# Weight columns 8 and 16 bytes apart in the two projections around a cross-attention

## The chip, the cores and the metric

One core of a Trainium2 chip runs the whole kernel. The metric is the device time of one execution in microseconds; the kernel before takes 1947.67 us, the median of three runs (1947.66 to 1947.83).

## The reference

One decoder block over 1024 tokens of width 1024: two recurrent branches, merged and projected, then cross-attention to 256 memory tokens, then a gated feed-forward network. The change concerns the cross-attention, which is, cut to what matters:

```python
def mem_cross_attention(n, m, w_xq, w_xkv, w_xo):
    q = (n @ w_xq).reshape(Bsz, S, XATTN_HEADS, XATTN_HEAD_DIM)
    k, v = jnp.split(m @ w_xkv, 2, axis=-1)
    ...
    s = jnp.einsum('bshd,bmhd->bhsm', q, k).astype(jnp.float32) * (XATTN_HEAD_DIM ** -0.5)
    p = jax.nn.softmax(s, axis=-1).astype(v.dtype)
    o = jnp.einsum('bhsm,bmhd->bshd', p, v).reshape(Bsz, S, D_MODEL)
    return o @ w_xo
```

`w_xq` and `w_xo` are 1024 x 1024 float32; there are four heads of 256.

## The kernel before, in words

Everything is float32 in and out, and matmuls run on fp32r operands. To keep precision each operand is split in two: `split` (L226) writes a high part with a ScalarE copy (L227) and a low part with VectorE's subtraction (recorded at L73, the line of a helper that records every two-input operation). A product is then three matmuls: high by high, high by low, low by high. The matmul itself is recorded at L51, a transpose at L55.

Five square matrices pass through one routine: the two branches' up-projections, the merge's output, the query projection (`w_xq`) and the attention's output projection (`w_xo`). Their weights are the left operand, the one that TensorE loads; class `Left` prepares them (L1190-1219). Each matrix is fetched in four DMAs of 256 columns into `raw` (L1197). From `raw` come eight tiles of 128 columns a matrix, one for each block of 128 output channels; a tile named `wd` holds both parts of the 8 blocks of the contraction, 128 partitions x 2 parts x 8 blocks x 128 columns (`slot(...)`, L1209). There are two such buffers, used in turn, so a tile is split into the buffer that the tile before the last leaves. In the text "weight tile" means one `wd`.

`dense` (L1236-1253) runs one matrix: for each of the 8 output blocks and each half of the tokens (512) it adds up 24 matmuls, 8 blocks x 3 products, in one PSUM bank `acc` (L1249); four such banks rotate. A tile is therefore read by 2 x 24 = 48 matmuls of 128 x 512, each with a weight load of its own (128 columns), and a matrix takes 384. The result goes to `post`, which empties the bank: in the query projection (`dense(3)`, L1407) a split into the attention's `hl` operand, in the output projection (`dense(4)`, L1537) the residual sum (`ga`), a store to memory, the statistics of the norm (`ssum`, `sq`) and a scaled copy `o` (L1534) for the feed-forward network, whose first operands (`B11h` and others) are split there too.

Between the two lies the attention (`Att`, L1412-1460): for each head and half, scores with 256 columns a matmul (`acc<-kvhl,hl`), the softmax on ScalarE and VectorE (`pe`, L1440), transposes on TensorE (`bank<-ident,pe`), a split of the transposed probabilities (`phl`), the sum over values (`bank<-phl,kvhl`), and a split of the result into `hl`, the right operand of the output projection.

The order is not written by hand: a scheduler places each instruction on its engine from its own estimate of times and from priorities. Splits of weights and the `post` steps are issued under `ahead` (L131), which raises their priority by 200 (L37). So TensorE already runs some matmuls of the output projection between the last heads' steps. Within an engine the instructions run in the order placed, each after the semaphores that it waits for.

Of the kernel before, what the change touches and what calls it, by code (L numbers as in the profile page):

```python
# [16 lines left out]
P = 128  # L17
TOK = 1024
D = 1024
NB = D // P  # L20
# [58 lines left out]
def block_kernel(ctx: ExitStack, tc: tile.TileContext, t: dict, out: bass.AP):  # L79
    nc = tc.nc  # L80
    now = [0.0]
    PE, ACT, SP = Tensor(nc.tensor, now), nc.scalar, nc.sync
# [39 lines left out]
    def acc():  # L122
        return ps.tile([P, 512], F32, name="acc", tag="acc", bufs=4)

    def bank(dt=F32):
        return ps.tile([P, 512], dt, name="bank", tag="bank", bufs=4)
# [7 lines left out]
    half = lambda j: slice(j * HALF, (j + 1) * HALF)  # L134
# [8 lines left out]
    def slot(key, shape=(P, 2, TOK), dt=F32, name="sl"):  # L143
        pl, n = slots[key]
        return pl.tile(list(shape), dt, name=name, tag="sl", bufs=n)
# [80 lines left out]
    def split(src, hi, lo, e=None):  # L226
        ACT.activation(hi, src, AF.Copy)  # L227
        sub(e or DVE, lo, src, hi)
# [5 lines left out]
    class Operands:  # L234
# [20 lines left out]
        def upto(s, n):  # L255

            while s.done < min(n, 7 * s.kh):
                next(s.steps)
                s.done += 1
# [287 lines left out]
    for k in range(NB):  # L547
        p = bank()
# [640 lines left out]

    class Left:  # L1190

        def __init__(s, mats):
            s.seq, s.raw, s.w, s.ring = [(W, u) for W in mats for u in range(4)], [], [], []
# [8 lines left out]
        def upto(s, n):  # L1204
            while len(s.w) < min(n, 2 * len(s.seq)):
                u, i = divmod(len(s.w), 2)
                s.load(u + 1)
                if len(s.w) < 2:
                    s.ring.append(slot("m", (P, 2, NB, P), F32R, name="wd"))  # L1209
                w = s.ring[len(s.w) % 2]  # L1210
                with ahead():
                    split(s.raw[u][:, :, i * P:(i + 1) * P], w[:, 0], w[:, 1])
                s.w.append(w)
                if i:
                    s.load(u + 3)

# [19 lines left out]
    def dense(no, ins, post, pre=lambda o, j: None, js=JS):  # L1236

        todo = [(o, j) for o in range(NB) for j in (js if o + 1 < NB else js[::-1])]
        got = [pre(*x) for x in todo[:2]]
        for n, (o, j) in enumerate(todo):  # L1240
            w = left[NB * no + o]
            if n + 2 < len(todo):
                got.append(pre(*todo[n + 2]))
            cur = got[n]
            p = acc()
            m = 0
            for k in range(NB):
                for a, b in ((0, 0), (0, 1), (1, 0)):
                    PE.matmul(p, w[:, a, k], ins[k][:, b, half(j)], start=m == 0, stop=m == 3 * NB - 1)  # L1249
                    m += 1  # L1250
            with ahead():
                post(o, j, p, cur)
            yield
# [122 lines left out]

    early = presum()
    run(dense(0, i_ys, post_ys, lambda o, j: gate(gs_d, o, j)), (fetch_gated(yg_d, sr_d, i_yg), 1.0), (waiting(early, 12), 1.0))
    run(dense(1, i_yg, post_yg, lambda o, j: (gate(gg_d, o, j), quad(ysg_d, o * P, 0, j))), (early, 1.1))
    run(dense(2, i_wo, residual(h1_d, s1, "norm_xattn", put_xq, 0.5), quad_of(xT_d)), (early, 1.1))  # L1380


# [88 lines left out]
    for n in range(len(at) + 2):  # L1471
        a = at[n] if n < len(at) else None
        b = at[n - 1] if 0 < n <= len(at) else None
# [277 lines left out]
```

## Time and profile before

| What | Value |
|---|---|
| timed runs, median (lowest, highest) | 1947.67 us (1947.66, 1947.83) |
| the profiled execution, its span | 1949.0 us |
| TensorE busy | 1916.2 us, 98% of the span |
| VectorE busy | 1298.5 us, 67% |
| ScalarE busy | 845.8 us, 43% |
| matmuls on weight tiles (all five matrices) | 1920, mean record 390 ns |
| their weight loads | 1920, mean record 188 ns |
| splits of weight tiles, ScalarE | 40, mean 1057 ns |
| splits of weight tiles, VectorE | 40, mean 1323 ns |
| query projection | about 1067 to 1156 us of the span |
| attention, with the output projection's start | 1156 to 1220 us |
| output projection, to its last matmul | 1198 to 1297 us |

The profiled execution's own time is its span, since nothing runs outside it in the record. PE is TensorE's matmul side, PEld its weight loads, which run beside the matmul before them; DVE is VectorE, ACT ScalarE, POOL GpSimd. A line of a view names the line of the code, the engine, the operation, and its operands as out<-in with their shapes. Matmuls' records overlap, so their mean is longer than the step from one to the next; the step is read from a row of the timeline, which gives a run of matmuls from the first start to the last end.

### The profile page before, as it was taken

What the parts mean: (1) busy time and instruction counts of PE and PEld (TensorE: products, weight loads), DVE (VectorE), ACT (ScalarE), POOL (GpSimd) and SP (SyncE); (2) the same over time, 40 slices, a digit from 0 to 9 for tenths busy, and PEclk for the clock granted to TensorE, in tenths of its full rate; (3) what the DMA queues carried; (4) which work ended last, traced back from release to release, by engine and by line L of the source; (5) the groups of instructions that cost most, each with busy time, mean ns of one, the idle gap of its engine ahead of it and who ended that gap; (6) DMA issues with size and microseconds to landing.
All of it is one profiled execution on the core that took longest, in us unless ns stands there. A gap on an engine that the chain in (4) does not pass through costs nothing.

```text
span 1949.0 us, 26264 instructions
## 1 busy us (share of the span) xinstructions
PE 1916.2 (98%) x9776; PEld 1615.6 (83%) x9776; DVE 1298.5 (67%) x1873; ACT 845.8 (43%) x1485; POOL 557.8 (29%) x428
## 2 busy tenths in 40 slices
PE   7999999999999999999999999999999999999998
PEld 7998787888878888788887888888888888888888
DVE  7766879877776764655534237677777777766566
ACT  7534564655553444643223235444333333345243
POOL 0012334345543231022433000006445544320002
PEclk9999999999999999999999999999999999999999
DMA  9423383446553653997675201442233224177463
GB/s 341 144 93 101 130 307 107 152 161 186 174 173 123 198 167 124 348 346 270 226 269 164 82 22 44 140 141 82 90 126 110 82 100 144 42 271 239 157 224 126
DMA packets 237875, 317.98 MB, mean 163 GB/s; under 512 B 16538, under 2 KB 156036, under 8 KB 237748
## 3 DMA queue, kind: packets, MB, share of 16 engines
q1 hardware_dynamic: 236020, 310.01, 47.4%
q10 hardware_dynamic: 1728, 6.29, 0.8%
q8 instruction: 77, 1.26, 0.3%
q14 instruction: 50, 0.41, 0.1%
HBM read 215.27 MB, written 100.99 MB: 162 GB/s over the span
## 4 chain that ended last, share of the span: by engine, by line
PE 43%; DMA 3%; POOL 2%; DVE 1%; issue 1%; ACT 1%; POOLq 0%; SPq 0%; DVEq 0%; ACTq 0%
PE acc L51 38%; PE bank L51 4%; DMA pre<-in_w_ffn_out_dram 1%; POOL pre L73 1%; DMA down_d<-pre 1%; PE bank L55 1%; POOL ssum L73 0%; DVE hl L73 0%; POOL sa L73 0%; DMA h_d<-ga 0%; DMA ga<-vm_d 0%; DVE wd L73 0%; ACT wd L227 0%; ACT sq L493 0%; DVE phl L73 0%
## 5 line engine op out<-in xcount | busy, mean ns | idle before, releaser
L51 PE MATMUL acc<-hl,wd 128*128 128x512 f32 x1920 | 440.4, 390 | 3.6 <-DVE wd L73 2.0
L51 PEld LDWEIGHTS acc<-hl,wd 128*128 128x128 f32 x1920 | 359.6, 188 | 80.7 <-DVE wd L73 3.3
L73 DVE TENSOR_TENSOR wlo<-raw,whi 128x512 fp32r<-128x512 f32 x272 | 236.4, 875 | 103.6 <-ACT whi L227 103.5
L227 ACT ACTIVATE whi<-raw 128x512 fp32r<-128x512 f32 x272 | 169.5, 629 | 247.6 <-PE acc L51 201.0
L73 DVE TENSOR_TENSOR o<-acc,o 128x512 f32<-128x512 f32 (+1 forms) x256 | 172.6, 676 | 108.8 <-PE acc L51 95.4
L51 PE MATMUL acc<-fs 128*128 128x512 f32 (+1 forms) x792 | 155.7, 356 | 0.1
L51 PEld LDWEIGHTS acc<-fs 128*128 128x128 f32 x792 | 130.7, 189 | 20.8 <-issue 0.5
L73 DVE TENSOR_TENSOR fs<-fr,fs 128x1024 fp32r<-128x1024 f32 (+1 forms) x84 | 98.9, 1217 | 36.5 <-ACT fs L227 36.4
L227 ACT ACTIVATE fs<-fr 128x1024 fp32r<-128x1024 f32 (+1 forms) x84 | 79.2, 982 | 95.9 <-PE acc L51 31.2
L73 POOL TENSOR_TENSOR raw<-raw,sa 128x512 f32<-128x512 f32 x44 | 57.1, 1297 | 207.8 <-DVE wlo L73 207.8
L73 POOL TENSOR_TENSOR sa<-raw 128x512 f32<-128x512 f32 x43 | 69.6, 1619 | 107.0 <-DMA raw<-in_w_in_dram 78.9
L227 ACT ACTIVATE whi<-sa 128x512 fp32r<-128x512 f32 x96 | 59.6, 626 | 93.7 <-PE acc L51 92.3
L73 DVE TENSOR_TENSOR wlo<-sa,whi 128x512 fp32r<-128x512 f32 x96 | 80.9, 843 | 13.7 <-ACT whi L227 12.7
L73 DVE TENSOR_TENSOR wd<-raw,wd 128x1024 fp32r<-128x1024 f32 x40 | 52.8, 1323 | 47.6 <-ACT wd L227 47.2
L73 POOL TENSOR_TENSOR rstd<-rstd,mhalf 128x4 f32<-128x4 f32 (+1 forms) x7 | 8.7, 1246 | 257.0 <-DVE rstd L73 257.0
L227 ACT ACTIVATE wd<-raw 128x1024 fp32r<-128x1024 f32 x40 | 42.2, 1057 | 90.4 <-PE acc L51 89.8
L51 PE MATMUL acc<-T4h,whi 128*128 128x512 f32 x192 | 76.3, 397 | 2.4 <-DVE o L73 2.4
L51 PE MATMUL acc<-B22h,wlo 128*128 128x512 f32 x192 | 75.7, 394 | 1.5 <-DVE wlo L73 1.5
L51 PE MATMUL acc<-T1h,whi 128*128 128x512 f32 x192 | 76.3, 397 | 0.0
L51 PE MATMUL acc<-T2h,whi 128*128 128x512 f32 x192 | 75.9, 395 | 0.0
L51 PE MATMUL acc<-T3h,whi 128*128 128x512 f32 x192 | 75.9, 395 | 0.0
L51 PE MATMUL acc<-B22h,whi 128*128 128x512 f32 x192 | 75.7, 394 | 0.0
(399 smaller groups left out, 4698.6 us busy)
## 6 DMA issues: line engine op xcount, KB each, us to landing
raw<-in_w_in_dram SPq DMA_DIRECT2D x26, 1024.0 KB, 5.9
raw<-in_w_ffn_in_dram SPq DMA_DIRECT2D x22, 1024.0 KB, 6.5
act_d<-o SPq DMA_DIRECT2D x77, 256.0 KB, 2.1
fr<-act_d SPq DMA_DIRECT2D x35, 512.0 KB, 7.9
pre<-in_w_ffn_out_dram SPq DMA_DIRECT2D x11, 1024.0 KB, 10.0
fr<-down_d SPq DMA_DIRECT2D x20, 512.0 KB, 3.9
down_d<-pre SPq DMA_DIRECT2D x33, 256.0 KB, 3.1
h_d<-ga SPq DMA_DIRECT2D x32, 256.0 KB, 3.1
```

Source lines behind the costliest of these rows:

```text
L51: return s.e.matmul(o, x, y, **kw)
L55: return s.e.transpose(o, x, i)
L73: return f(*a, **kw)
L227: ACT.activation(hi, src, AF.Copy)
```

## The change

A table `STEP` gives each of the five matrices a distance between neighbouring columns of its weight tiles, in elements of 4 bytes: 1 for the first three, which stay as they were, 2 for the query projection and 4 for the output projection. With step n the tile's 8 blocks are laid in groups of n: the columns of n blocks take turns, so column c of block k lies n elements after column c - 1. The tile keeps its size. The weight load of a matmul then reads 128 elements that lie 8 or 16 bytes apart in each partition, 1024 or 2048 bytes from end to end, where it read 512 bytes in a piece.

The split writes into that layout. With step 1 it remains one ScalarE and one VectorE instruction of 128x1024. With a larger step it is done block by block: 8 and 8 instructions of 128x128, which read from `raw` as before and write 128 elements with the step. This concerns the 16 tiles of the two matrices: 16 + 16 instructions become 128 + 128.

```diff
+        STEP = (1, 1, 1, 2, 4)
...
-                w = s.ring[len(s.w) % 2]
+                n = s.STEP[len(s.w) // NB]
+                w = s.ring[len(s.w) % 2].rearrange("p x k c -> p x (k c)").rearrange("p x (a c b) -> p x a b c", c=P, b=n)
                 with ahead():
-                    split(s.raw[u][:, :, i * P:(i + 1) * P], w[:, 0], w[:, 1])
-                s.w.append(w)
+                    for a, b in ((a, b) for a in range(NB // n) for b in range(n)) if n > 1 else ((slice(0, NB), 0),):
+                        k = a * n + b if n > 1 else a
+                        split(s.raw[u][:, k, i * P:(i + 1) * P], w[:, 0, a, b], w[:, 1, a, b])
+                s.w.append([[w[:, x, k // n, k % n] for k in range(NB)] for x in range(2)])
...
-                    PE.matmul(p, w[:, a, k], ins[k][:, b, half(j)], start=m == 0, stop=m == 3 * NB - 1)
+                    PE.matmul(p, w[a][k], ins[k][:, b, half(j)], start=m == 0, stop=m == 3 * NB - 1)
```

What it moves, engine by engine. The orders of GpSimd and of the DMA queues stay, and TensorE's but for a few neighbours that swap places in the attention. Line numbers after L1210 are 3 higher. In the rows below the number is the row's place, then line, operation, operands, shape, and how many stand in a row.

VectorE at the end of the merge's output projection and the start of the query projection, before; `hl<-ga` is the second part of the query projection's right operand, `ga<-acc` the emptying of a bank:

```order
868 L73 SCALAR_TENSOR_TENSOR hl<-ga,cols,hl 128x512
869 L73 SCALAR_TENSOR_TENSOR ga<-acc,ga 128x512
870 L73 TENSOR_TENSOR wd<-raw,wd 128x1024
871 L73 SCALAR_TENSOR_TENSOR hl<-ga,cols,hl 128x512
872 L73 SCALAR_TENSOR_TENSOR ga<-acc,ga 128x512
873 L73 SCALAR_TENSOR_TENSOR hl<-ga,cols,hl 128x512
874 L73 SCALAR_TENSOR_TENSOR ga<-acc,ga 128x512
875 L73 TENSOR_TENSOR wd<-raw,wd 128x1024
876 L73 SCALAR_TENSOR_TENSOR hl<-ga,cols,hl 128x512
```

The same place now:

```order
868 L73 SCALAR_TENSOR_TENSOR hl<-ga,cols,hl 128x512
869 L73 TENSOR_TENSOR wd<-raw,wd 128x128 x6
870 L73 SCALAR_TENSOR_TENSOR ga<-acc,ga 128x512
871 L73 TENSOR_TENSOR wd<-raw,wd 128x128 x2
872 L73 SCALAR_TENSOR_TENSOR hl<-ga,cols,hl 128x512
873 L73 SCALAR_TENSOR_TENSOR ga<-acc,ga 128x512
874 L73 SCALAR_TENSOR_TENSOR hl<-ga,cols,hl 128x512
875 L73 TENSOR_TENSOR wd<-raw,wd 128x128 x6
876 L73 SCALAR_TENSOR_TENSOR ga<-acc,ga 128x512
877 L73 TENSOR_TENSOR wd<-raw,wd 128x128 x2
878 L73 SCALAR_TENSOR_TENSOR hl<-ga,cols,hl 128x512
```

Where a whole subtraction stood between the last `ga` and the last `hl`, two of its eight pieces stand now; the other six have moved ahead of that `ga`.

ScalarE in the attention's tail, before; `phl` is the split of the transposed probabilities, `hl<-bank` that of the values' sum, `o` and `ssum` belong to the output projection's first result:

```order
655 L227 ACTIVATE phl<-bank 128x512 x2
656 L227 ACTIVATE hl<-bank 128x512 x2
657 L227 ACTIVATE phl<-bank 128x512 x2
658 L227 ACTIVATE hl<-bank 128x512 x4
659 L1534 ACTIVATE o<-ga,cols 128x512
660 L490 ACTIVATE ssum<-ga 128x512
661 L227 ACTIVATE wd<-raw 128x1024
```

The same place now:

```order
656 L227 ACTIVATE wd<-raw 128x128 x3
657 L227 ACTIVATE phl<-bank 128x512 x2
658 L227 ACTIVATE hl<-bank 128x512 x2
659 L227 ACTIVATE wd<-raw 128x128
660 L227 ACTIVATE phl<-bank 128x512 x2
661 L227 ACTIVATE hl<-bank 128x512 x2
662 L227 ACTIVATE wd<-raw 128x128 x2
663 L227 ACTIVATE hl<-bank 128x512 x2
664 L1537 ACTIVATE o<-ga,cols 128x512
665 L490 ACTIVATE ssum<-ga 128x512
666 L227 ACTIVATE wd<-raw 128x128 x2
```

The copy of the output projection's third weight tile came after the first result; its pieces now begin six steps earlier, among the splits of the attention's last two rounds, each piece as soon as its part of the buffer has been read. VectorE's pieces follow in the same way.

## The prediction, made before the changed kernel had run

> **What bounds the kernel now.** I read the page's totals and its chain first, then the granted clock, then the chain of waits from the query projection on, and then busy time by stage.
>
> ```profile
> span 1949.0 us, 26264 instructions
> ...
> PE 1916.2 (98%) x9776; PEld 1615.6 (83%) x9776; DVE 1298.5 (67%) x1873; ACT 845.8 (43%) x1485; POOL 557.8 (29%) x428
> ...
> PE 43%; DMA 3%; POOL 2%; DVE 1%; issue 1%; ACT 1%; POOLq 0%; SPq 0%; DVEq 0%; ACTq 0%
> ```
> ```profile
> core 0: 1949.0 us, clock 0.998
> ```
> ```profile
> 1074.73 9.36 PE acc L51 x40
> ...
> 1087.37 77.08 PE acc L51 x370
> ...
> 1215.13 2.49 PE acc L51 x11
> 1217.63 2.72 PE bank L51 x12
> 1220.35 85.00 PE acc L51 x375
> ```
>
> TensorE is busy 98% of the span at full clock, and in both changed stages the chain is its matmuls. The query projection runs here from about 1067 to 1156 us; the output projection's matmuls begin at 1198, between the attention's last pieces, and end at 1297. The next view gives busy time by stretch (PE, PEld, DVE, ACT, POOL); the line after it is the output projection's group of matmuls from 1198 to 1297.
>
> ```profile
> core 0: us, PE busy (x) PEld busy (x) DVE busy (x) ACT busy (x) POOL busy (x), PEclk, DMA share, GB/s
> 1066.00:1157.00 91.00, 90.85 (x411) 75.23 (x410) 26.56 (x32) 21.52 (x32) 6.25 (x5) 1.00 0.21 68
> ...
> 1198.00:1220.00 22.00, 22.00 (x107) 18.36 (x106) 10.59 (x24) 8.87 (x19) 0.00 (x0) 1.00 0.15 48
> 1220.00:1297.00 77.00, 77.00 (x341) 63.78 (x340) 48.73 (x71) 35.53 (x57) 0.00 (x0) 1.00 0.42 140
> ```
> ```profile
> L51 PE MATMUL acc<-hl,wd 128*128 128x512 f32 x384 | 88.4, 390 | 0.0
> ```
>
> TensorE has 0.15 us of idle in the query projection and none in the output projection, while VectorE is busy 26.56 of 91 and 48.73 of 77 us. So only two things can move the time: TensorE's pace on these 2 x 384 matmuls, or a wait that opens where none is now. The profiled execution's own time is its span, 1949.0 us; the timed runs' median, 1947.67, lies 1.3 us under it, and I carry that offset along. 0.2% of it, 3.9 us, is about what a measurement of this kernel can tell from no change.
>
> **The change: TensorE.** Count and order of the matmuls, and all DMAs, stay. What changes is how each weight load reads its 128 columns: 4 bytes apart before (512 bytes in all), 8 in the query projection (a stretch of 1024), 16 in the output projection (2048). No weight load in this trace reads columns apart, so the price has to be bounded. A load costs nothing while it fits beside the matmul before it; the question is how long one takes and how much room it has. TensorE's timeline gives the pace (start, time, count), and the groups by form the mean record of the second kind:
>
> ```profile
> 1059.68 14.89 PE L51 MATMUL acc<-hl,wd 128*128 128x512 f32 x65
> ...
> 1156.50 7.96 PE L51 MATMUL acc<-kvhl,hl 128*128 128x256 f32 x65
> ```
> ```profile
> L51 PE MATMUL acc<-kvhl,hl 128*128 128x256 f32 x192 | 25.9, 288 | 0.0
> ```
>
> The weight tiles' own records (min/median/max in ns), and who waited for them:
>
> ```profile
> L51 PEld LDWEIGHTS acc<-hl,wd x1920: 186/188/193, 801.9 to 1296.6; 128*128 128x128 f32 x192
> L51 PE MATMUL acc<-hl,wd x1920: 387/389/504, 801.9 to 1296.8; 128*128 128x512 f32 x192
> L227 ACT ACTIVATE wd<-raw x40: 1039/1061/1065, 800.8 to 1275.2; 128x1024 fp32r<-128x1024 f32 x40
> L73 DVE TENSOR_TENSOR wd<-raw,wd x40: 1211/1225/2319, 803.2 to 1276.3; 128x1024 fp32r<-128x1024 f32 x40
> ...
>   PEld acc L51: 6.2, 7
>   PE acc L51: 3.3, 5
> ```
>
> A matmul's record (389 ns) is longer than its pace, since neighbours overlap: a row's time is 64 steps and one last record. So 512 columns go at (14.89 - 0.39) / 64 = 0.2266 us. The attention's scores stream 256 columns, and each has a load of its own too: (7.96 - 0.288) / 64 = 0.1199 us. The difference, 106.7 ns, is what 256 columns cost; 512 then cost 213.4, and 13.2 ns a matmul are left over that don't grow with the columns. And a contiguous load takes at most 119.9 ns of TensorE's path, or the scores could not go at their pace. Against 226.6 that leaves 106.7 ns: a load stays hidden until it takes 226.6 / 119.9 = 1.89 times its bound. (The load's record, 188 ns, holds latency, as the matmul's does, and is no price.)
>
> So the term is zero while the load grows by less than that, and 384 x (load - 226.6 ns) for each stage beyond. Below zero it goes only if part of the 13.2 ns falls away, for which I see no reason (rival 4); upward the ends are a load that grows with the stretch it spans and a stream held up by it (rivals 1 and 2). I take zero, because the room is nearly the whole bound once more and the nearest row, the score at half the width, shows a load fully beside its matmul.
>
> [...]
>
> **The change: the splits.** Each of the 16 weight tiles of these two stages was split by one ScalarE copy (1.061 us) and one VectorE subtraction (1.225 us) of 128x1024; now each is 8 pieces of 128x128. The trace has no such piece writing apart; the nearest rows are 128x128 pieces of other lines, the cheapest and the dearest of each engine:
>
> ```profile
> L911 ACT ACTIVATE bt<-bank 128x128 f32<-128x128 f32 x16 | 4.3, 266 | 19.3 <-PE bank L55 18.1 <-DMA xbc_d<-cv 1.2
> L921 ACT ACTIVATE e<-csb,cs 128x128 f32<-128x128 f32 x120 | 36.7, 389 | 19.0 <-DMA csb<-cs_d 18.9
> L73 DVE TENSOR_TENSOR bank<-bank,triu 128x128 f32<-128x128 f32 x16 | 4.6, 290 | 0.6 <-ACT bt L911 0.6
> L73 DVE TENSOR_TENSOR rd<-sq 128x128 f32<-128x128 f32 x16 | 9.7, 607 | 0.0
> ```
>
> ScalarE: 8 x 0.266 = 2.1 us a tile, at most 8 x 0.389 = 3.1; VectorE: 8 x 0.290 = 2.3 us, at most 8 x 0.607 = 4.9. I take the lower ones (a plain copy and a two-input operation, as here), so +1.1 us each a tile, +17 us on each engine in all, at worst +33 and +58. Their cover is TensorE: a tile serves 48 matmuls, 48 x 0.2266 = 10.9 us. VectorE in the output projection is busy 48.73 of 77 us, so 6.9 of every 10.9; with +1.1 it is 8.0, at worst 6.9 + 3.6 = 10.5, still under. ScalarE: 35.53 of 77, 5.0 of 10.9, at worst 7.1. A tile is split while the one before it is used, so from the last read of its buffer it has 10.9 us, and needs 2.3 us now, some 5 at worst with its pieces one after the other. Term: zero; with the cover gone it would be up to 3.6 us a tile.
>
> **The change: waits and their order.** A whole split waited for the last matmul that reads the old tile; a piece waits for the last one that reads that piece. Three matmuls read each, so in a tile's last use pieces come free every 3 x 0.2266 = 0.68 us and the pieces can start up to 5 us earlier, but then stand on ScalarE and VectorE ahead of other work that must wait behind them. In the query projection that is the next output's evacuation, which with four accumulation banks of 24 x 0.2266 = 5.4 us each may come 16 us late before TensorE stops. In the attention's tail pieces stand ahead of the probabilities' splits, for which TensorE waits at once. The rows of that place, by engine:
>
> ```profile
> 1202.27 2.43 PE L51 MATMUL acc<-hl,wd 128*128 128x512 f32 x10
> 1204.54 1.03 PE L55 MATMUL bank<-ident,pe 128*128 128x128 f32 x8
> 1205.88 2.89 PE L51 MATMUL bank<-phl,kvhl 128*128 128x512 f32 x12
> ```
> ```profile
> 1205.18 1.09 ACT L227 ACTIVATE phl<-bank 128x512 fp32r<-128x512 f32 x2 [2.11 <-PE bank L55]
> ```
> ```profile
> 1205.81 1.29 DVE L73 TENSOR_TENSOR phl<-bank,phl 128x512 fp32r<-128x512 f32 x2 [2.02 <-ACT phl L227]
> ```
>
> Three pieces now stand before this split. The matmuls that free them are at the latest in the ten that end as the transposes begin, 1204.54; the third piece is then done on ScalarE by 1204.54 + 0.27 (0.39) = 1204.9 and on VectorE by 1205.2 (at worst 1204.54 + 0.39 + 0.61 = 1205.5), before 1205.18 and 1205.81, where both engines sat idle 2.1 and 2.0 us. Term: zero, at worst some tenths of a us at each of the last three heads' halves, under 1 us. Against that stands what can be won, the one wait of TensorE at the query projection's start, where fewer pieces now stand ahead of the last operand's split:
>
> ```profile
> 1074.73 9.36 PE L51 MATMUL acc<-hl,wd 128*128 128x512 f32 x40 [0.15 <-DVE hl L73]
> ```
>
> 0.15 us at most. Sum: 1949.0 + 0 + 0 + 0 us, less the offset: **1947.6 us**, in its own case between 1946.5 and 1949.5.
>
> **Rival 1: the load outgrows its cover (slower).** It decides from 1.89 times the bound. First form: only the wide step of the output projection is slowed, to about twice: at most 0.2398 us, 13.2 ns over the pace, 384 x 0.0132 = +5.1 us, 1952.7; at 2.3 times 49 ns and +18.9 us. Second form: time goes with the stretch spanned, twice at 8 bytes (+5.1 us) and four times at 16: (0.4796 - 0.2266) x 384 = +97.2, together about 2050 us. [...] Against: twice is nearly all covered, and four times needs a read that gives nothing to its neighbour. Chances 0.13 and 0.06. [...]
>
> **Rival 2: the loads' reads hold up the stream (slower).** The 13.2 ns may be what a load's reads take from the matmul beside it. If they go with the stretch, 8 bytes add 13.2 ns and 16 bytes 39.6: 384 x 0.0132 = 5.1 and 384 x 0.0396 = 15.2 us, 1967.9. For it: nothing else in the trace accounts for the rest. Against: the shortest matmul (387 ns) is no shorter than the median (389), though seven loads and five matmuls came after a wait, without their usual neighbour. Chance 0.15; a weaker form, under 3.9 us, counts with the forecast. [...]
>
> **Rival 3: pieces wait in order ahead of something due (slower).** If writing apart makes pieces dear and late, each of 16 tiles might hold TensorE for 0.3 us, half a worst VectorE piece: +4.8 us, 1952.4. Against: the 2 us of idle before the tightest splits. Chance 0.05.
>
> **Rival 4: faster.** Only if the 13.2 ns shrink: by half over 768 matmuls, -5.1 us, 1942.5. Nothing in the trace speaks for it. Chance 0.04.
>
> **The numbers.** Forecast 0.57; slower 0.13 + 0.06 + 0.15 + 0.05 = 0.39; faster 0.04. The range reaches from 1945 to 1969: to rival 2's time, because stopping short of it would leave out 0.15 + 0.06 and part of rival 1; what it leaves out is rival 1's second form and most of rival 4. The forecast's own range is 1946.5 to 1949.5.
>
> **What would show it.** Right: in the changed profile both stages' matmuls go on at 0.2266 us each, the projections end at the same times as before, and VectorE's and ScalarE's busy time rise by about 17 us each. Load records may grow (from 188 ns) with no effect. Rival 1 shows as a pace above 0.2266 in the output projection alone (first form) or far above it there; rival 2 as a pace above it in both, one to three; rival 3 as idle of TensorE ended by a split of the weights or probabilities. A pace of over 0.237 in either stage (384 x 0.0102 = 3.9 us) makes the prediction wrong.

## The result, and the profile after

| | Before | After |
|---|---|---|
| timed runs, median (lowest to highest) | 1947.66 us (1946.01 to 1948.07), 6 runs | 1953.34 us (1949.73 to 1958.05), 6 runs |
| ratio, 95% interval | | 1.0031 (1.0018 to 1.0044), so +3.5 to +8.6 us |
| the profiled execution's span | 1949.0 us | 1956.3 us |

The change made the kernel slower, by a few microseconds but clearly. The forecast was no change, 1946.5 to 1949.5 us; the time lies outside that, and inside the wide range that was drawn to take in the slower rivals. The profiled execution of the changed kernel is the longest of its six, so the sums below are made inside it and set against the interval of the timed runs.

The page of the changed kernel, totals. Busy time is up for PE, PEld, DVE and ACT; the matmuls are as many as before:

```profile
span 1956.3 us, 26621 instructions
...
PE 1921.8 (98%) x9776; PEld 1636.2 (84%) x9776; DVE 1319.9 (67%) x1985; ACT 871.0 (45%) x1597; POOL 555.8 (28%) x428
```

Busy time by stage (PE, PEld, DVE, ACT, POOL, granted clock), in the stages' new places:

```profile
1066.00:1160.00 94.00, 92.89 (x407) 76.88 (x406) 38.13 (x100) 34.19 (x96) 6.68 (x6) 1.00 0.21 68
...
1224.00:1304.00 80.00, 80.00 (x342) 79.92 (x342) 55.67 (x107) 44.60 (x93) 0.00 (x0) 1.00 0.41 135
```

The second row is the one to read. TensorE ran its last 340 or so matmuls of the output projection in 80 us, where it took 77, and its load side, with 16 bytes between columns, was busy all of that time (79.92 of 80); before it was busy 63.78 of 77. In the first row TensorE has 1.11 us of idle where it had 0.15.

TensorE's timeline, one row from the middle of the query projection, one from the output projection, and the place of the wait:

```profile
1075.81 11.01 PE L51 MATMUL acc<-hl,wd 128*128 128x512 f32 x46 [1.11 <-ACT hl L1371]
...
1094.75 62.46 PE L51 MATMUL acc<-hl,wd 128*128 128x512 f32 x267
...
1224.50 80.06 PE L51 MATMUL acc<-hl,wd 128*128 128x512 f32 x340
```

The row of the output projection before:

```profile
1220.18 77.00 PE L51 MATMUL acc<-hl,wd 128*128 128x512 f32 x339
```

With the rule of the prediction (a row's time is its steps and one last record) the pace is (62.46 - 0.394) / 266 = 0.2333 us at 8 bytes and (80.06 - 0.396) / 339 = 0.2350 us at 16. Before, the output projection went at (77.00 - 0.390) / 338 = 0.2267 us, and the prediction's row ahead of the query projection gives 0.2266. The records of the weight tiles in the query projection (first three rows) and in the output projection say what grew (min/median/max, ns):

```profile
L51 PE MATMUL acc<-hl,wd x391: 389/394/504, 1065.8 to 1159.8; 128*128 128x512 f32 x196
L51 PEld LDWEIGHTS acc<-hl,wd x390: 187/193/198, 1066.0 to 1159.8; 128*128 128x128 f32 x195
L227 ACT ACTIVATE wd<-raw x73: 299/317/440, 1065.7 to 1158.6; 128x128 fp32r<-128x128 f32 x73
...
L51 PEld LDWEIGHTS acc<-hl,wd x384: 308/310/330, 1202.1 to 1303.9; 128*128 128x128 f32 x192
L51 PE MATMUL acc<-hl,wd x384: 387/396/601, 1202.3 to 1304.2; 128*128 128x512 f32 x192
L227 ACT ACTIVATE wd<-raw x48: 415/434/452, 1207.4 to 1281.8; 128x128 fp32r<-128x128 f32 x48
L73 DVE TENSOR_TENSOR wd<-raw,wd x48: 371/391/404, 1207.9 to 1282.7; 128x128 fp32r<-128x128 f32 x48
```

A load at 8 bytes has a record only 5 ns longer (193 against 188), one at 16 bytes 122 ns longer (310). Three terms come out of these rows: 384 x 6.7 ns = 2.6 us in the query projection, 384 x 8.4 ns = 3.2 us in the output projection, and 1.11 - 0.15 = 1.0 us of wait at the query projection's start; 6.8 us in all. The last load of a weight tile starts 7.3 us later than before (1303.9 against 1296.6), but the first one of all, long before the change has any effect, 1.0 us later (802.9 against 801.9). So 6.3 us belong to the stretch between, 0.5 less than the three terms add up to.

Where the wait comes from stands in the chain of the changed kernel just ahead of it (start, time, what):

```profile
1071.82 0.22 ACT wd L227
...
1073.31 1.09 DVE wd L73 x5
1074.40 0.61 DVE ga L73
1075.01 0.02 issue
1075.04 0.73 ACT hl L1371
1075.77 0.04 issue
1075.81 11.01 PE acc L51 x46
```

The pieces that have moved ahead of the last `ga` hold it up: VectorE works through five of them in a row before the sum that everything waits for.

### The profile page after: what moved, and what is told of

Its sections match the earlier page's. It is cut to its first block, busy times and chain, and to the rows that moved or that the text cites. A ratio compares the mean times of both kernels' runs of the same rounds, so it can differ in the third digit from the quotient of the medians.

```text
span 1956.3 us, 26621 instructions
## 1 busy us (share of the span) xinstructions
PE 1921.8 (98%) x9776; PEld 1636.2 (84%) x9776; DVE 1319.9 (67%) x1985; ACT 871.0 (45%) x1597; POOL 555.8 (28%) x428
## 4 chain that ended last, share of the span: by engine, by line
PE 43%; DMA 3%; POOL 2%; issue 2%; DVE 1%; ACT 1%; POOLq 0%; SPq 0%; DVEq 0%; ACTq 0%
PE acc L51 38%; PE bank L51 4%; POOL pre L73 1%; DMA pre<-in_w_ffn_out_dram 1%; DMA h_d<-ga 1%; DMA down_d<-pre 1%; POOL ssum L73 0%; PE bank L55 0%; POOL sa L73 0%; DMA ga<-vm_d 0%; DVE hl L73 0%; DVE wd L73 0%; ACT hl L1371 0%; ACT sq L493 0%; DVE ga L73 0%
## 5 line engine op out<-in xcount | busy, mean ns | idle before, releaser
L51 PE MATMUL acc<-hl,wd 128*128 128x512 f32 x1920 | 446.1, 393 | 4.9 <-ACT wd L227 2.0
L51 PEld LDWEIGHTS acc<-hl,wd 128*128 128x128 f32 x1920 | 380.6, 213 | 67.4 <-DVE wd L73 3.1
L227 ACT ACTIVATE wd<-raw 128x128 fp32r<-128x128 f32 (+1 forms) x152 | 67.8, 481 | 77.5 <-PE acc L51 76.1
L73 DVE TENSOR_TENSOR wd<-raw,wd 128x128 fp32r<-128x128 f32 (+1 forms) x152 | 76.0, 523 | 37.2 <-ACT wd L227 35.2
```

The costliest lines, as they stand in the source:

```text
L51: return s.e.matmul(o, x, y, **kw)
L73: return f(*a, **kw)
```

## The experiments

Theory A, formed from these rows: the loads laid apart slow TensorE's pace, by 6.7 ns a matmul at 8 bytes and 8.4 at 16, and the pieces only add the wait at the query projection's start. Rival B: the pieces, their number and place, slow TensorE.

**Pieces without the layout.** In this run the columns lie 4 bytes apart again and the tile is laid out as it was before; `STEP` only says which matrices are split in pieces. Against the kernel before, cut to the split:

```diff
...
-                    split(s.raw[u][:, :, i * P:(i + 1) * P], w[:, 0], w[:, 1])
+                    for k in range(NB) if n > 1 else (slice(0, NB),):
+                        split(s.raw[u][:, k, i * P:(i + 1) * P], w[:, 0, k], w[:, 1, k])
```

> The splits of the last two matrices stay in 8 + 8 pieces of 128x128, but the layout is the old one: columns 4 bytes apart. Theory A (the strided loads slow TensorE's pace; the pieces only move the wait at the query projection's start): both projections at the old pace, 226.6 ns a matmul, TensorE's wait at the start of the query projection near 1.1 us instead of 0.15, so about +1.0 us, 1948.6. Rival B (the pieces themselves, their number and their place beside the matmuls, slow TensorE): a pace of 233 to 235 ns and +5 to +6 us, as in the changed kernel.

Measured: 1948.98 us against 1947.99, ratio 1.0005 (0.9995 to 1.0015). TensorE's timeline:

```profile
1073.19 9.16 PE L51 MATMUL acc<-hl,wd 128*128 128x512 f32 x32 [2.08 <-ACT hl L1370]
...
1089.69 68.41 PE L51 MATMUL acc<-hl,wd 128*128 128x512 f32 x301
```

The pace of the query projection is (68.41 - 0.389) / 300 = 0.2267 us, the old one, and that of the output projection is 0.2267 too (315 matmuls in 71.56 us). The wait is there, 2.1 us in this execution, where about 1.1 was expected. Both are as theory A has them.

**The layout without pieces.** One instruction of each engine splits a tile, writing with the step; TensorE's order is that of before. Against the changed kernel:

```diff
-                    for a, b in ((a, b) for a in range(NB // n) for b in range(n)) if n > 1 else ((slice(0, NB), 0),):
-                        k = a * n + b if n > 1 else a
-                        split(s.raw[u][:, k, i * P:(i + 1) * P], w[:, 0, a, b], w[:, 1, a, b])
+                    split(s.raw[u][:, :, i * P:(i + 1) * P].rearrange("p (a b) c -> p a b c", b=n), w[:, 0], w[:, 1])
```

> The changed layout (8 and 16 bytes), but each tile is split by one ScalarE and one VectorE instruction as before, which write with the step; TensorE's order is that of before. Theory A: 233.3 ns a matmul in the query projection and 235.0 in the output projection, 384 x 6.7 = +2.6 and 384 x 8.4 = +3.2 us, together +5.8, 1953.4; the wait at the query projection's start back at 0.15 us. Rival B: the old pace of 226.6 ns in both and no change, 1947.7.

Measured: 1954.70 us against 1947.99, ratio 1.0031 (1.0019 to 1.0042). TensorE's timeline, and then the chain at the start of the attention:

```profile
1094.74 60.59 PE L51 MATMUL acc<-hl,wd 128*128 128x512 f32 x259
...
1160.60 1.70 PE L51 MATMUL acc<-kvhl,hl 128*128 128x256 f32 x12 [0.96 <-DVE hl L73]
...
1224.78 75.59 PE L51 MATMUL acc<-hl,wd 128*128 128x512 f32 x321
```
```profile
1155.14 2.10 ACT wd L227
...
1157.27 2.08 DVE wd L73
```

Paces: (60.59 - 0.394) / 258 = 0.2333 and (75.59 - 0.395) / 320 = 0.2350 us. So the layout alone makes the slower pace, and rival B is out. The splits' writes lie apart in this run too, so one might blame them and not the loads. The trace of the changed kernel speaks against it: from 1100 to 1150 us all 213 steps from one matmul's start to the next take 232 to 235 ns, though ScalarE is busy only 16.7 and VectorE 16.9 of these 50 us, so that for a third of the time neither writes anything. The wait at the query projection's start is gone, as theory A has it; what theory A did not say is a new one of 1.0 us in the first scores, since a whole split that writes at 16 bytes takes ScalarE 2.10 and VectorE 2.08 us (1.06 and 1.23 contiguous) and stands ahead of the last query operand.

**Each stage alone.** `STEP = (1, 1, 1, 2, 1)` and `STEP = (1, 1, 1, 1, 4)`:

> Only the query projection has the step (8 bytes, in pieces); the output projection is as before. Theory A: +2.6 us of pace and about +1.0 us of the wait at its start, 1951.2; output projection at 226.6 ns. Rival B: the same +2.6 if it is the pieces, so this run does not part them by itself; it gives the share of the first stage.

> Only the output projection has the step (16 bytes, in pieces); the query projection is as before. Theory A: +3.2 us, 1950.9, with 235.0 ns a matmul there, 226.6 ns and a wait of 0.15 us in the query projection. If the shares of the two stages do not add up to the whole change (+5.7), there is a third part, which I do not know.

Measured against 1947.99: 1954.21 us, ratio 1.0027 (1.0018 to 1.0036), for the query projection; 1952.28 us, ratio 1.0021 (1.0013 to 1.0030), for the output projection. Both are slower by themselves: by 3.5 to 7.0 and 2.5 to 5.8 us. The expected +3.6 and +3.2 lie in the intervals, the first at its very edge. The two medians add up to more (+10.5) than the whole change (+5.7), but the ends of the two intervals add up to 6.0 and 12.8, which overlaps the change's own 3.5 to 8.6: the times neither show a third part nor rule one out. In the profiles each stage alone has the slower pace, as expected: 0.2333 us in the query projection of the first run (237 matmuls in 55.46 us) and (75.59 - 0.396) / 320 = 0.2350 us in the output projection of the second, while the other stage of each stays at 0.2267. The wait at the start is 1.3 us in the first run; in the second it is 0.4, where 0.15 was expected:

```profile
1071.66 10.54 PE L51 MATMUL acc<-hl,wd 128*128 128x512 f32 x44 [1.28 <-ACT hl L1371]
```
```profile
1221.71 75.59 PE L51 MATMUL acc<-hl,wd 128*128 128x512 f32 x321
```

**How long a load takes.** The five stages get different steps, `STEP = (16, 8, 1, 2, 4)`; for 16 the two parts are interleaved as well. The first form of this run:

> All five matrices get a step, split by whole instructions: 64 bytes between columns (w_up_ssd, high and low parts interleaved too), 32 bytes (w_up_gla), 4 (w_o), 8 (w_xq), 16 (w_xo). Theory A1 (from 16 bytes on each column is a read of its own and more distance costs nothing more): 235.0 ns a matmul at 64 and at 32 bytes too, 226.6 at 4, 233.3 at 8; 384 x (8.4 x 3 + 6.7) ns = +12 us, about 1960. Rival A2 (a load's time goes with the stretch that it spans): 16 bytes is then just at the limit of the cover, 32 bytes takes about 2 x 230 = 460 ns a matmul and 64 bytes 920, +90 and +266 us, about 2310.

Its one time was 2016.68 us (1946.49 before). In it, and in the two runs with narrow matmuls below, the first nine tiles are split one after the other before the first matmul that uses any of them, into the two buffers in turn. All but the last two are overwritten unused, so the products of the first matrix are of other weights, and its stage begins late (at 838 us, where it was 802). That adds to the time; the pace is read inside a stage. The same steps with each tile split when it is due:

> The five matrices at 64, 32, 4, 8 and 16 bytes between columns, each tile split by whole instructions when it is due. Theory A1 (from 16 bytes on each column is a read of its own, and more distance costs little more): 384 x (236.6 - 226.6) = 3.8 us at 64 bytes, 384 x (245.4 - 226.6) = 7.2 at 32, 2.6 at 8 and 3.2 at 16, together +16.8, near 1964.5, and some us more if the splits, twice as long from 16 bytes on, come late. Rival A2 (time goes with the stretch spanned): +350 us.

Measured: 1968.93 us against 1948.45, ratio 1.0102 (1.0083 to 1.0122). A1's times hold and A2, hundreds of microseconds, is out; whether each column is then a read of its own, no run shows. The 4 us over A1's 1964.5 fit the late splits that it allowed for: from 800 to 1310 us TensorE waits 8.8 us in the profiled execution, the longest of the four, and 3.9 before. TensorE's timeline in the second matrix (32 bytes) and the loads of the first (64 bytes):

```profile
898.77 91.42 PE L51 MATMUL acc<-hl,wd 128*128 128x512 f32 x374
```
```profile
L51 PEld LDWEIGHTS acc<-hl,wd x392: 293/302/334, 804.6 to 897.8; 128*128 128x128 f32 x196
```

The pace is (91.42 - 0.405) / 373 = 0.2440 us at 32 bytes; at 64 it is 0.2364 (the mean step from 810 to 890 us), less than at 32. The medians of the load records in this run are 310 ns at 16 bytes, 329 at 32 and 302 at 64: four times the distance takes no longer.

How much of the 235.0 ns is the load's own shows when the matmul beside it is short. Each matmul of these stages is cut into two of 256 columns, or four of 128, each with its load:

```diff
-                    PE.matmul(p, w[a][k], ins[k][:, b, half(j)], start=m == 0, stop=m == 3 * NB - 1)
+                    for c in range(0, HALF, 256):
+                        PE.matmul(p[:, c:c + 256], w[a][k], ins[k][:, b, j * HALF + c:j * HALF + c + 256], start=m + c == 0, stop=m == 3 * NB - 1 and c + 256 == HALF)
```

> The steps of the run with 64, 32, 4, 8 and 16 bytes, but every matmul of these five stages is cut into two of 256 columns, each with its own load. Theory A5 (at 16 bytes the load itself takes about 230 to 235 ns and is the limit): 235 ns a matmul of 256 columns at 16, 32 and 64 bytes, 120.0 at 4 bytes, and at 8 bytes 120 + 6.7 = 127, as the load is not yet doubled. Rival A6 (the load is still beside its matmul and only adds some ns to the stream): 120 + 8.4 = 128 ns at 16 bytes. Rival A2: 235 at 8 bytes too, 460 and more from 32 bytes.

Measured: 2270.23 us (one run; 1946.49 before). TensorE's timeline, at 32, 4, 8 and 16 bytes in this order:

```profile
1079.68 70.52 PE L51 MATMUL acc<-hl,wd 128*128 128x256 f32 x292
...
1229.78 50.44 PE L51 MATMUL acc<-hl,wd 128*128 128x256 f32 x419
...
1308.55 61.69 PE L51 MATMUL acc<-hl,wd 128*128 128x256 f32 x512
...
1450.76 39.48 PE L51 MATMUL acc<-hl,wd 128*128 128x256 f32 x169
```

The paces are 0.2410, 0.1200, 0.1202 and (39.48 - 0.394) / 168 = 0.2327 us. At 16 bytes a matmul of half the width takes nearly as long as a whole one: the load is the limit, at 0.233 us, 1.94 times the bound of 119.9 ns. A5 is right there, A6 out. Of the 8.4 ns that a wide matmul pays, this leaves about 6 to the load's overrun (0.2327 against 0.2266) and about 2 that no run explains. The first matrix's stage (64 bytes) speaks against the writes too: no tile is split in it from 850 to 1005 us, and a matmul of 256 columns still takes 0.223 us, where it takes 0.120 at 4 bytes. At 8 bytes A5 was wrong: nothing is added (every step in an undisturbed stretch is 120 ns, as at 4 bytes), so that load fits in 0.120 us like the contiguous one.

> As before with four matmuls of 128 columns, each with its own load: the stream is then 53 ns long, so the pace is the load's own time if that is longer. Theory A5: 120 ns at 4 bytes if a contiguous load takes the bound read from the attention's scores (67 if the bound was far too high), 127 at 8, 235 at 16, 32 and 64 bytes. Rival A6: 67 to 75 ns at 4 bytes and 128 or less at 16.

Measured: 3274.65 us (one run). The granted clock fell, so the 4 byte number can't be read as meant. Stages at 4 and at 16 bytes, first by busy time with the clock in the third column from the end, then TensorE's timeline:

```profile
1558.00:1886.00 328.00, 328.00 (x1539) 328.00 (x1539) 34.20 (x44) 31.07 (x44) 20.15 (x14) 0.50 0.11 36
...
2260.00:2630.00 370.00, 370.00 (x1589) 366.72 (x1588) 74.10 (x101) 55.57 (x82) 0.00 (x0) 0.53 0.12 40
```
```profile
1559.68 300.57 PE L51 MATMUL acc<-hl,wd 128*128 128x128 f32 x1408
...
2273.54 326.72 PE L51 MATMUL acc<-hl,wd 128*128 128x128 f32 x1400
```

At half the clock a matmul of 128 columns with a contiguous load takes 300.57 / 1408 = 0.213 us, and one with a load at 16 bytes (clock 0.53 in the row above) 326.72 / 1400 = 0.233 us, the same as one of 256 columns at full clock. So between these two runs the time of the load at 16 bytes, 0.233 us, went neither with the granted clock nor with the width of the matmul beside it. What sets it, no run shows.

**One part of the tile apart.** Where the 6.7 ns at 8 bytes fall. High and low part get steps of their own, in five pairs; the high part is copied whole, the low part subtracted block by block:

```diff
-        STEP = (1, 1, 1, 2, 4)
+        STEP = ((1, 2), (2, 1), (1, 1), (1, 4), (4, 1))
```

> Only one of the two parts of a tile is laid apart: matrices 1 to 5 have (high, low) at steps of (4, 8), (8, 4), (4, 4), (4, 16), (16, 4) bytes; of each three matmuls two load the high part and one the low. Theory A3 (each load laid apart costs its own 6.7 or 8.4 ns and its neighbours nothing): means of 228.8, 231.1, 226.6, 229.4 and 232.2 ns a matmul, and the single steps show which matmul pays. Rival A4 (the load at 16 bytes is over its cover only because the loads follow each other without a gap): with a 4 byte load between, the 16 byte stages stay at 226.6 to 228 ns, and 8 bytes too.

Measured: 1958.84 us (one run; 1946.49 before). TensorE's timeline, rows from the stages (8, 4), (4, 16) and (16, 4):

```profile
889.74 88.59 PE L51 MATMUL acc<-hl,wd 128*128 128x512 f32 x379
...
1088.61 69.68 PE L51 MATMUL acc<-hl,wd 128*128 128x512 f32 x299
...
1226.02 79.29 PE L51 MATMUL acc<-hl,wd 128*128 128x512 f32 x339
```

Their paces are 0.2333, 0.2325 and 0.2334 us, that of the stage (4, 8) is 0.2315, and neither theory holds (A3 expected 231.1, 229.4, 232.2 and 228.8 ns). Two loads of three at 8 bytes cost as much as three, one of three at 16 bytes 5.9 ns of the full 8.4: the cost is not each load's own, nor does a 4 byte load between hide it. The single steps say who pays: in the stage (8, 4) all 257 steps from 900 to 960 us take 232 to 235 ns, though every third load there is contiguous. A load laid apart is paid for by the matmuls around it too.

**How it goes with the width.** Two runs asked whether the 13.2 ns that a contiguous matmul needs beside its columns, and the 6.7 ns at 8 bytes, are fixed or grow with the columns. The first cuts each matmul unevenly:

> Every matmul of the five stages is cut in two, each with its own load: 384 + 128 columns in matrices 1 (4 bytes), 2 (8 bytes) and 5 (16 bytes), 320 + 192 columns in matrices 3 (4 bytes) and 4 (8 bytes). It asks what the 13.2 ns beside the columns are and where the 6.7 ns at 8 bytes come from. Theory A7 (both are fixed per matmul; a contiguous load takes 120 ns, which hides them at 256 columns or fewer): pairs of 173.3 + 120 = 293 ns at 4 bytes and 180 + 120 = 300 at 8 bytes with 384 + 128; 146.7 + 120 = 267 and 153.3 + 120 = 273 with 320 + 192. Rival A8 (they grow with the columns, a stream that goes at 226.6 / 512 and at 233.3 / 512 ns a column): 170.0 + 120 = 290 and 175.0 + 120 = 295; 141.6 + 120 = 262 and 145.8 + 120 = 266. At 16 bytes both: two loads of 233, a pair of 467.

Measured: 2115.46 us (one run). Timeline of the pairs of 384 + 128 at 4, at 8 and at 16 bytes (the view names a row by its first form):

```profile
799.63 110.75 PE L51 MATMUL acc<-hl,wd 128*128 128x384 f32 x769 [0.83 <-ACT wd L227]
...
911.76 110.46 PE L51 MATMUL acc<-hl,wd 128*128 128x384 f32 x743
...
1294.70 165.77 PE L51 MATMUL acc<-hl,wd 128*128 128x384 f32 x710
```

A pair takes about 288, 297 and 467 ns by these rows. At 16 bytes that is what both theories expected, two loads of 233. At 4 and 8 bytes the expectations were 293 and 300, or 290 and 295, and neither fits: a pair mixes two widths and two loads. But the pair at 8 bytes does take some 9 ns more than the one at 4 (with 320 + 192 it is 268 against 259). So the second run gives each stage one width:

```diff
-                    PE.matmul(p, w[a][k], ins[k][:, b, half(j)], start=m == 0, stop=m == 3 * NB - 1)
+                    d = HALF if m in (0, 3 * NB - 1) else (384, 384, 448, 320, 320)[no]
+                    PE.matmul(p[:, :d], w[a][k], ins[k][:, b, j * HALF:j * HALF + d], start=m == 0, stop=m == 3 * NB - 1)
```

> Of each output's 24 matmuls the first and the last have 512 columns and the 22 between only the first 384, 384, 448, 320, 320 (matrices 1 to 5), so the rest of those products is left out and the values differ; steps of 4, 8, 8, 8 and 4 bytes. One width a stage, so its pace is read without pairs. Theory A7 (13.3 ns fixed per matmul at 4 bytes, 20.0 at 8, nothing of it growing with the columns): 173.3 ns at 384 columns and 4 bytes, 180.0 at 384 and 8, 206.7 at 448 and 8, 153.3 at 320 and 8, 146.7 at 320 and 4. Rival A8 (0.4427 and 0.4557 ns a column): 170.0, 175.0, 204.2, 145.8, 141.7. If 8 bytes cost 6.7 ns only at 512 columns and nothing from 448 down, it is neither.

Measured: 1865.83 us (one run, with work left out). Timeline rows inside one output each, at 384 columns and 4 bytes, 384 and 8, 448 and 8, 320 and 8, 320 and 4:

```profile
844.67 2.93 PE L51 MATMUL acc<-hl,wd 128*128 128x384 f32 x16
...
913.22 3.11 PE L51 MATMUL acc<-hl,wd 128*128 128x384 f32 x17
...
987.81 4.23 PE L51 MATMUL acc<-hl,wd 128*128 128x448 f32 x20
...
1066.77 2.66 PE L51 MATMUL acc<-hl,wd 128*128 128x320 f32 x17
...
1179.63 2.36 PE L51 MATMUL acc<-hl,wd 128*128 128x320 f32 x15
```

With the records' means (334, 336, 364, 310 and 309 ns) the paces are 173.1, 173.4, 203.5, 146.9 and 146.5 ns. At 4 bytes A7 is right: about 13 ns beside the columns at 320, 384 and 512 alike. At 8 bytes nothing is added at 320 and 384, about 3.5 ns at 448 (200.0 would be A7's contiguous pace) and 6.7 at 512, which is neither theory. Among matmuls of one width the cost of 8 bytes falls on wide ones, and begins between 384 and 448 columns. The uneven pairs, which pay 9 ns with 384 + 128, show that this does not carry over to mixed widths.

**Both waits avoided.** The tiles of the query projection are split whole, those of the output projection in pieces:

```diff
+                    if st == 4:
+                        for k in range(NB):
+                            split(s.raw[u][:, k, i * P:(i + 1) * P], w[:, 0, k // st, k % st], w[:, 1, k // st, k % st])
+                    else:
+                        split(s.raw[u][:, :, i * P:(i + 1) * P].rearrange("p (a b) c -> p a b c", b=st), w[:, 0], w[:, 1])
```

> The changed layout, 8 and 16 bytes; the tiles of the query projection are split whole, those of the output projection in 8 + 8 pieces. Theory A: the pace is unchanged, 233.3 and 235.0 ns (+5.8 us), and TensorE waits neither at the query projection's start (0.2 us, against 1.1 to 2.1 in the runs whose pieces stand there) nor in the attention's first scores (against 1.0 in the run that splits the 16 byte tiles whole): near 1953.5 to 1954. Rival B2: the waits come from the strided writes and not from the way of splitting, and one of them stays.

Measured: 1952.64 us against 1948.45, ratio 1.0020 (1.0010 to 1.0030), +2.0 to +5.8 us. What TensorE waits for from 1060 to 1300 us (total, times, longest):

```profile
PE bank L55 <- DVE phl L73: 0.4, 1, 0.4
```

TensorE's timeline in the two stages:

```profile
1094.61 60.59 PE L51 MATMUL acc<-hl,wd 128*128 128x512 f32 x259
...
1224.68 73.72 PE L51 MATMUL acc<-hl,wd 128*128 128x512 f32 x313
```

The paces are (60.59 - 0.394) / 258 = 0.2333 and (73.72 - 0.395) / 312 = 0.2350 us. Both waits are gone, the slower pace stays: the waits come from how the tiles are split, the rest from how they lie. The two paces' +5.8 us lie at the upper end of the interval. It is still slower than before, and no run here that does the whole work beats the kernel before.

## Why the prediction was wrong, point by point

- **TensorE's term was not zero.** The step that failed is the sentence "a load costs nothing while it fits beside the matmul before it". At 8 bytes the load does fit, in 0.120 us as the run with 256 columns shows, and yet the matmul of 512 columns pays 6.7 ns: 2.6 us. That is like rival 2 as far as the stream is slowed beside a load that is itself hidden, but not its size (13.2 ns) and not its law, since matmuls of 256 to 384 columns in a row pay nothing. Neither pace passed the 0.237 us that the prediction named as the sign of being wrong: that sign took each stage by itself, and two stages under it add up to 5.8 us.
- **At 16 bytes the load outgrew its cover.** The term's own condition, 1.89 times the bound, was right and was crossed: 0.233 us is 1.94 times. (The 119.9 ns are themselves only an upper bound of the contiguous load.) Rival 1's first form is what happened there, with +8.4 ns (3.2 us) where it allowed at most 13.2 (5.1). I had given it 0.13, because twice seemed nearly all covered; 0.233 us against 0.2266 is nearly all covered indeed, but "nearly" times 384 is over half of the whole effect. That the measured 1953.3 us lie so near this form's 1952.7 is luck, since other terms make up the sum. The rival's second form, time by the stretch spanned, is refuted by the run with 32 and 64 bytes. That a load at 16 bytes takes twice the bound, 0.2398 us, from which the 1952.7 come, was an estimate: no run shows that figure, and what the runs showed in its place is 0.233 us. Beside 256 columns the pace is 0.120 us at 4 and at 8 bytes, and 0.223 to 0.241 from 16 to 64.
- **The start of the query projection.** The prediction read there that fewer pieces stand ahead of the last `hl`, a gain of at most 0.15 us. It left out of the sum the six that had moved ahead of the `ga` from which that `hl` is made; they wait for ScalarE's pieces and pass the delay on. TensorE's wait there is 1.1 us in this profile, and 2.1 and 1.3 in two other runs with pieces there. It is none in the two runs that split these tiles whole into the new layout, and 0.4 in the run that left this stage as it was. This is rival 3's mechanism at another place.
- **What held.** The splits' longer time stays beside TensorE (+25.2 us on ScalarE and +21.4 on VectorE; I had 17 each), and the pieces in the attention's tail cost nothing that shows. The pieces alone, with the old layout, cost no more than 2.9 us by the timed interval, and in the profile only the wait.
- **What stays open.** Why 8 bytes cost a wide matmul 6.7 ns and a narrower one nothing. It is not the pieces, not the splits' writes and not a cost of each load by itself. A longer load is not seen beside 256 columns, but the uneven pairs, dearer by 9 ns at 8 bytes, leave room for a part that shows only beside a very short matmul; more the runs don't say. Open too are the 2 ns at 16 bytes that the load's overrun leaves over.

## What to carry to other kernels

A weight load that hides beside its matmul has a margin, and the margin is worth measuring as a number before the layout is touched: here at least 107 ns (226.6 - 119.9), used up and a little more by 16 bytes between columns (0.233 us against 0.2266). A hidden load is still not always free: eight bytes apart cost nothing here in rows of matmuls of 256 to 384 columns, 3% in rows of 512, and 3% in pairs of 384 and 128. When one instruction is cut into pieces, look at what each piece now stands ahead of, and at what is made from that, not only at the last step before the waiting engine.

## What the runs showed of the hardware that was not expected

- Writing at 16 bytes slows ScalarE and VectorE as well: 1.06 to 2.08 us (nearly double) and 1.23 to 2.08 us (1.7 times) for 128x1024, in the run with whole splits. The medians of its query projection (8 bytes) are 1127 and 1227 ns, 6% over and equal to the contiguous time; the longest of each row is the first tile at 16 bytes:

```profile
L227 ACT ACTIVATE wd<-raw x7: 1127/1127/2058, 1074.9 to 1143.9; 128x1024 fp32r<-128x1024 f32 x7
L73 DVE TENSOR_TENSOR wd<-raw,wd x7: 1226/1227/2025, 1076.1 to 1146.0; 128x1024 fp32r<-128x1024 f32 x7
```

- The granted clock fell to between 0.50 and 0.53 in the stages whose matmuls had 128 columns beside each load, though TensorE was busy throughout (328.00 of 328 us at 4 bytes); with 256 columns beside a load of 0.233 us it stayed at 1.00, as the busy time of that run's 16 byte stage shows:

```profile
1430.00:1610.00 180.00, 180.00 (x784) 178.63 (x783) 60.91 (x81) 44.52 (x63) 0.00 (x0) 1.00 0.20 66
```
